# A two-layer trunk of attention and experts: output products gated as a sum, and the mixers' large GpSimd work moved to VectorE

## Chip, cores and metric

The kernel runs on one core of a Trainium2 chip. The metric is the device time of one execution in microseconds (us). A core has five engines that run side by side, each with its own queue in program order: TensorE (PE, matrix products; PEld is its loading of weights), VectorE (DVE), ScalarE (ACT), GpSimd (POOL) and SyncE (SP), which here only issues transfers (DMA). Data lie in SBUF; products come out in PSUM, which has banks of 128 rows by 512 fp32 values. [...]

## Reference

512 positions of width 1024 go through two layers. Each layer is a mixer (layer 0 differential attention, layer 1 banded attention), followed by a mixture of 16 experts, of which each position uses two:

```python
for i in range(DEPTH):
    mod = silu_c @ ada_w[i] + ada_b[i]
    sh1, sc1, g1, sh2, sc2, g2 = [m[:, None, :] for m in jnp.split(mod, 6, axis=-1)]
    h = rms_norm(x, norm_mix_g[i]) * (1.0 + sc1) + sh1
    y = diff_attention(h, ...) if i % 2 == 0 else chunked_attention(h, ...)   # both end in o @ w_o
    x = x + g1 * y
    h = rms_norm(x, norm_ffn_g[i]) * (1.0 + sc2) + sh2
    x = x + g2 * grouped_moe(h, router_w, router_bias, moe_w_gate[i], moe_w_up[i], moe_w_down[i])
```

The products that matter here are `h @ w_qkv` (1024 x 3072), `o @ w_o` (1024 x 1024) with its gate g1, and the adaLN product that gives `mod`. The routing takes sigmoid scores, picks one of four groups of experts and two experts in it.

## The kernel before

All order is written out by hand: the program issues instructions engine by engine in the order of the Python code, and each engine runs its own in that order.

**Weights** arrive as tiles of 128 x 2048 (1 MB) through rings of buffers. `ring.take()` hands out the next tile that has been requested, `ring.done` frees it, and that issues SP's next transfer. To get more than one pass of precision, `split_half` (L330) takes half a tile apart: hi is a copy of reduced precision on ScalarE (L337), lo is the rest, a subtraction (L338) on the engine that `eng` names, VectorE or GpSimd. Three products follow: hi by hi, hi by lo, lo by hi.

**A mixer** walks a list BLOCKS of 12 projection blocks (three for each of four parts q of the heads, L663) and four output blocks ("wo", one for each part, L679). `main_block(n)` runs a block, and at its ticks (every 8 matmuls, or every output group of six) drops in side work: the two splits for the next block, adaLN tiles (`ada_next`), small operations from the lists `bg` and `fin_bg`, and TensorE's transposes of adaLN results from `pe_bg`. Beside it runs `att_stream(q)`, the attention of one part: scores (L747), softmax pieces (VectorE L752, ScalarE L755, VectorE L763 to L775), transposes (L785) and the product with the values (L802, L806). `run_streams` picks which stream goes next by the costs that they yield. Blocks 3 to 11 have the attention of parts 0 to 2 beside them, the output blocks 12 to 14 that of part 3. In layer 0 three output groups are held back to follow it (`held`).

**Engines of the side work.** In the projections one of the two lo parts of a block is GpSimd's, in the output blocks the second one too. The output weights of every part are first multiplied by g1, on GpSimd (L336, two operations of 128 x 1024 per part), so that the products can be added straight to the residual rows `xs` (VectorE, L681): one addition for each part, each of four tiles of rows and each of two column halves, 32 a layer. An adaLN tile is multiplied by the conditioning and accumulated: its first half in one VectorE operation (L431), its second half on ScalarE (L433) and GpSimd (L435). At the layer boundary `first_parts` splits the first weights of layer 1 with both lo parts on GpSimd, while VectorE runs the reciprocal root of the norm (L167 to L173, tiny operations on 128 x 4) and scales the rows (L486); then come the transposes (L538).

**The tail** of a mixer is the output block of part 3 run together with the routing's preparation; then the routing follows, a chain of small VectorE operations with a few small matmuls between (L1082, L1141, L1171), a flag that says whether an expert overflows (a branch, L1389), the gathering of rows and the first expert unit (L1339). The experts' weights come as a stream of 1 MB transfers through three rings.

## Time and profile before

| what | value |
|---|---|
| median of three runs | 1315.2 us (1313.8 to 1316.43) |
| profiled execution | 1313.69 us, span 1311.8 us |
| mean granted clock | 0.947 |
| TensorE busy | 1166.7 us, 89% of the span |
| VectorE, ScalarE, GpSimd busy | 819.5, 617.6, 326.9 us |
| DMA | 327.59 MB, mean 250 GB/s |

The span runs from the first to the last instruction of the profiled execution. Busy times are sums over one engine's instructions; where two engines need each other, the busy shares alone do not tell which sets the time, the idle time before an instruction and its releaser do. The layers lie one after the other: start up to 58 us, layer 0's mixer to 364, routing to 402, experts to 690, layer boundary, layer 1's mixer from 708 to 985, routing, experts to the end.

### The profile page before, as it was taken

What the parts mean: (1) busy time and instruction counts of PE and PEld (TensorE: products, weight loads), DVE (VectorE), ACT (ScalarE), POOL (GpSimd) and SP (SyncE); (2) the same over time, 40 slices, a digit from 0 to 9 for tenths busy, and PEclk for the clock granted to TensorE, in tenths of its full rate; (3) what the DMA queues carried; (4) which work ended last, traced back from release to release, by engine and by line L of the source; (5) the groups of instructions that cost most, each with busy time, mean ns of one, the idle gap of its engine ahead of it and who ended that gap; (6) DMA issues with size and microseconds to landing.
All of it is one profiled execution on the core that took longest, in us unless ns stands there. A gap on an engine that the chain in (4) does not pass through costs nothing. (4 is left out here: it accounts for less than half of the span.)

```text
span 1311.8 us, 19539 instructions
## 1 busy us (share of the span) xinstructions
PE 1166.7 (89%) x7070; PEld 840.4 (64%) x7070; DVE 819.5 (62%) x1800; ACT 617.6 (47%) x1204; POOL 326.9 (25%) x307
## 2 busy tenths in 40 slices
PE   5998899978677999999896999997996899998988
PEld 1677778866565555455576988877775645544565
DVE  3458877779857355254676577856775726544475
ACT  3335556533346254344656455543334634443472
POOL 3114331323242011112103223332525101112211
PEclk7999899989897999999997999998998899999989
DMA  8685565526157699999952343440624879999984
GB/s 291 239 303 215 207 211 192 193 67 230 54 203 298 248 410 404 408 409 410 388 201 77 114 144 112 145 144 33 240 100 179 317 287 402 403 412 403 408 350 138
DMA packets 81937, 327.59 MB, mean 250 GB/s; under 512 B 10663, under 2 KB 35783, under 8 KB 52136
## 3 DMA queue, kind: packets, MB, share of 16 engines
q1 hardware_dynamic: 71176, 302.33, 59.1%
q0 software_dynamic: 10656, 23.93, 7.0%
q8 instruction: 57, 0.93, 0.3%
q14 instruction: 48, 0.39, 0.1%
HBM read 312.53 MB, written 23.15 MB: 256 GB/s over the span
## 5 line engine op out<-in xcount | busy, mean ns | idle before, releaser
L663 PE MATMUL mm<-wlo,hT_hi 128*128 128x256 f32 x704 | 202.9, 288 | 0.8 <-DVE wlo L338 0.8
L663 PE MATMUL mm<-whi,hT_lo 128*128 128x256 f32 x704 | 203.3, 289 | 0.0
L663 PE MATMUL mm<-whi,hT_hi 128*128 128x256 f32 x704 | 202.5, 288 | 0.0
L338 POOL TENSOR_TENSOR wlo<-ring,whi 128x1024 fp32r<-128x1024 f32 x37 | 90.0, 2434 | 375.4 <-ACT whi L337 280.6
L338 DVE TENSOR_TENSOR wlo<-mring,whi 128x1024 fp32r<-128x1024 f32 x116 | 135.6, 1217 | 26.3 <-ACT whi L337 25.6
L755 ACT ACTIVATE p<-p,st 128x128 f32<-128x128 f32 (+3 forms) x128 | 71.0, 555 | 158.4 <-DVE st L752 158.4
L663 PEld LDWEIGHTS mm<-wlo,hT_hi 128*128 128x128 f32 x704 | 135.6, 193 | 12.6 <-issue 9.8
L337 ACT ACTIVATE whi<-mring 128x1024 fp32r<-128x1024 f32 x116 | 119.1, 1056 | 52.2 <-DMA mring<-in_moe_w_gate_dram 20.3
L663 PEld LDWEIGHTS mm<-whi,hT_hi 128*128 128x128 f32 x704 | 135.8, 193 | 5.9 <-issue 2.4
L663 PEld LDWEIGHTS mm<-whi,hT_lo 128*128 128x128 f32 x704 | 135.8, 193 | 5.6 <-issue 4.0
L337 ACT ACTIVATE whi<-ring 128x1024 fp32r<-128x1024 f32 x104 | 107.1, 1049 | 17.7 <-POOLq L1389 6.7
L338 DVE TENSOR_TENSOR wlo<-ring,whi 128x1024 fp32r<-128x1024 f32 x67 | 87.4, 1323 | 44.1 <-ACT whi L337 41.0
L1216 POOL DMA_INDIRECT xb<-y,idx x28 | 56.5, 2016 | 169.0 <-DVE y L1383 94.7
L1210 POOL DMA_INDIRECT hg<-hs,idx x24 | 25.9, 1080 | 283.7 <-DVE wg L1200 129.4
L1301 ACT ACTIVATE hgTf<-tr,mcol 128x128 f32<-128x128 f32 x128 | 48.5, 455 | 88.8 <-PE tr L1296 68.4
L679 PE MATMUL mm<-whi,o 128*128 128x512 f32 x256 | 87.4, 423 | 2.4 <-DVE xs L681 2.1
L1345 PE MATMUL s<-mring,hgTw 128*64 128x512 f32 x224 | 61.2, 614 | 8.2 <-DMA mring<-in_moe_w_up_dram 8.2
L752 DVE CUSTOM_DVE_ANT_0 p<-s,T 128x128 f32<-128x128 f32 (+3 forms) x128 | 57.7, 484 | 13.9 <-PE s L747 12.3
L1339 PE MATMUL mm<-whi,hgTh 128*128 128x512 f32 x128 | 57.6, 450 | 9.6 <-ACT hgTh L1315 9.5
L1376 DVE SCALAR_TENSOR_TENSOR th<-th,s 128x512 f32<-128x512 f32 x24 | 16.4, 684 | 77.4 <-PE s L1345 59.5
L666 ACT ACTIVATE raw<-mm 128x256 f32<-128x256 f32 x88 | 33.0, 376 | 66.8 <-PE mm L663 66.6
L1339 PE MATMUL s<-wlo,hgTh 128*128 128x512 f32 x128 | 52.1, 407 | 8.8 <-DVE wlo L338 8.8
(354 smaller groups left out, 2654.5 us busy)
## 6 DMA issues: line engine op xcount, KB each, us to landing
mring<-in_moe_w_up_dram SPq DMA_DIRECT2D x54, 1024.0 KB, 15.1
mring<-in_moe_w_gate_dram SPq DMA_DIRECT2D x48, 1024.0 KB, 18.4
mring<-in_moe_w_down_dram SPq DMA_DIRECT2D x42, 1024.0 KB, 21.0
ring<-in_ada_w_dram SPq DMA_DIRECT2D x40, 1024.0 KB, 6.6
ring<-in_moe_w_down_dram SPq DMA_DIRECT2D x22, 1024.0 KB, 19.3
ring<-in_moe_w_gate_dram SPq DMA_DIRECT2D x16, 1024.0 KB, 15.5
ring<-in_a_w_qkv_dram SPq DMA_DIRECT2D x24, 512.0 KB, 5.9
ring<-in_b_w_qkv_dram SPq DMA_DIRECT2D x24, 512.0 KB, 5.5
```

Source lines behind the costliest of these rows:

```text
L337: A.activation(hi, raw[:, s], AF.Copy)
L338: eng.tensor_sub(lo, raw[:, s], hi.bitcast(F32))
L663: P.matmul(ps[:, :256], a[:, j, ts_], b[:, w], start=(k == 0), stop=(k == 23))
L666: A.activation(raw[:, t, :], ps[:, :256], AF.Copy)
L679: P.matmul(ps, a[:, j, ts_], b[:, ns], start=(k == 0), stop=(k == 5))
L752: V.tensor_tensor_reduce(out=p[:, :nk], in0=pst[m][:, :nk], in1=T[:, 512 - nk:], scale=-1.0, scalar=3e38, op0=OP.add, op1=OP.min, accum_ou ...
L755: A.activation(p[:, :nk], p[:, :nk], AF.Exp, scale=-1.0, bias=st_[:, m:m + 1], accum_out=st_[:, 2 + m:3 + m])
L1210: G.indirect_dma_start(out=hgs[e % HG], out_offset=None, in_=hs, in_offset=bass.IndirectOffsetOnAxis(ap=idx[:, e:e + 1], axis=0), bounds_c ...
L1216: G.indirect_dma_start(out=xb, out_offset=bass.IndirectOffsetOnAxis(ap=ix[0:n], axis=0), in_=y[0:n], in_offset=None, bounds_check=S - 1, o ...
L1301: A.activation(f, b[:, 128 * (i % 4):128 * (i % 4) + 128], AF.Identity, scale=mcol[:, l, 3, i:i + 1], bias=mcol[:, l, 2, i:i + 1])
L1339: P.matmul(o, a, b, start=(first and i == 0), stop=(last and i == 2))
L1345: P.matmul(b[s, :], lhs[:, s], w[h], start=first, stop=last)
```

## The change

Six things are edited.

1. The output weights' tiles now hold a half of the columns (`wo_item`). A new `wo_block` runs the output products of parts 0 to 2 together: for each column half and each pair of row tiles it opens two banks and adds the 18 matmuls of three parts into each. The sum is multiplied by g1 and added to `xs`, both on VectorE. Splits of the six half tiles are placed at fixed group numbers (`todo`; two of them already in block 11). Only part 3's weights are still multiplied by g1, on VectorE.
2. `split_half` puts lo on VectorE, except where the tail asks for GpSimd. The adaLN tile's second half takes VectorE's one operation too.
3. `first_parts` puts its lo parts off until the rows are scaled.
4. `pe_bg` gets an empty entry, so that adaLN transposes come a tick later; layer 0 does not flush it any more before part 3's attention; seven groups are held back instead of three; tiles of part 3 come from a new pool T["y"].
5. `keep_busy(n)` runs n matmuls 128x512 in fp32 whose result nobody reads, five after the routing's transpose, four after its next-to-last small products.
6. At the routing's end two hi parts come before the overflow flag's branch, and their lo parts after the second gather.

```diff
-            G.tensor_mul(raw[:, s], raw[:, s], scale)
+            r3 = raw[:, s].rearrange("p (j f) -> p j f", j=2)
+            V.tensor_mul(r3, r3, scale[:, None, 512 * k:512 * k + 512].to_broadcast([128, 2, 512]))
         A.activation(hi, raw[:, s], AF.Copy)
-        eng.tensor_sub(lo, raw[:, s], hi.bitcast(F32))
+        if later is None:
+            eng.tensor_sub(lo, raw[:, s], hi.bitcast(F32))
+        else:
+            later.append(lambda: eng.tensor_sub(lo, raw[:, s], hi.bitcast(F32)))
...
-            if k == 0:
-                if j == ej[0]:
-                    V.tensor_scalar(acc[k], w, cj, None, op0=OP.mult)
-                else:
-                    V.scalar_tensor_tensor(acc[k], w, cj, acc[k], op0=OP.mult, op1=OP.add)
+            if j != ej[0]:
+                V.scalar_tensor_tensor(acc[k], w, cj, acc[k], op0=OP.mult, op1=OP.add)
+            elif k:
+                A.activation(acc[k], w, AF.Copy, scale=cj)
             else:
-                A.activation(acc[k] if j == ej[0] else w, w, AF.Copy, scale=cj)
-                if j != ej[0]:
-                    G.tensor_add(acc[k], acc[k], w)
+                V.tensor_scalar(acc[k], w, cj, None, op0=OP.mult)
...
+    def keep_busy(n):
+
+        b = bank("s", 2)
+        for t in range(n):
+            P.matmul(b, ident, xs[:, t % NT, 0:512], start=True, stop=True)
+
+    first_low = []
...
-        parts = [split_half(raw, k, eng=eng) for k in range(2)]
-        ring.done(raw)
+        parts = [split_half(raw, k, later=first_low) for k in range(2)]
+        first_low.append(lambda: ring.done(raw))
...
+        while first_low:
+            first_low.pop(0)()
...
-                if BLOCKS[i][0] == "wo":
-                    parts.append(split_half(raw, k, state["g1"], eng=(G if k else V)))
-                else:
-                    parts.append(split_half(raw, k, eng=(V if k else G)))
+                parts.append(split_half(raw, k, state["g1"] if BLOCKS[i][0] == "wo" else None))
...
+        def wo_block():
+
+            wo_split(2, 0)
+            todo = {3: (0, 1), 8: (1, 1), 10: (2, 1)}
+            nxt = load_split(15)
+            n_y = 0
+            for nb in range(2):
+                ns = slice(512 * nb, 512 * nb + 512)
+                for t2 in range(0, NT, 2):
+                    banks = [bank("mm", 2) for _ in range(2)]
+                    for q in range(3):
+                        hi, lo = wo_parts[q, nb]
+                        ohi, olo = oT[q]
+                        for t, ps in zip((t2, t2 + 1), banks):
+                            ts_ = slice(128 * t, 128 * t + 128)
+                            k = 0
+                            for j in range(2):
+                                w = slice(512 * j, 512 * j + 512)
+                                for a, b in ((ohi, hi), (olo, hi), (ohi, lo)):
+                                    P.matmul(ps, a[:, j, ts_], b[:, w], start=(q == 0 and k == 0), stop=(q == 2 and k == 5))
+                                    k += 1
+                            if q == 2:
+                                V.tensor_mul(ps, ps, state["g1"][:, ns])
+                                V.tensor_add(xs[:, t, ns], xs[:, t, ns], ps)
+                            n_y += 1
+                            bg_step(3)
+                            if pe_bg and n_y % 3 == 0:
+                                pe_bg.pop(0)()
+                            if n_y in todo:
+                                wo_split(*todo[n_y])
+                            if n_y in (14, 22):
+                                nxt[1](n_y // 22)
+                            yield 1300.0
+            state["cur"] = nxt
...
-            held = 3 if l == 0 and n == 4 else 0
+            held = 7 if l == 0 and n == 4 else 0
...
-                while pe_bg:
+                while l and pe_bg:
...
         P.transpose(lgb[:, 0:128], T["lsb"], ident)
+        keep_busy(5)
...
         G.dma_start(g2, bc_row(modd, l * 6 * D + 5 * D, D))
+        keep_busy(4)
         places()
+        low = []
+        split_next(later=low)
+        split_next(later=low)
         overflow()
...
         gather(1)
-        split_next()
-        split_next()
+        for o in low:
+            o()
```

GpSimd's queue at the end of layer 0's mixer, before. `g` is the gate g1, `ring` a weight tile, `T` and `rowsA` the bias rows of the attention; the last rows of lo parts lie in the tail:

```order
L336 TENSOR_TENSOR ring<-ring,g_2455 128x1024 x2
L338 TENSOR_TENSOR wlo<-ring,whi 128x1024
L606 MEMSET T 64x64
L608 DMA T<-rowsA 64x512
L609 DMA T<-rowsA 64x448
L336 TENSOR_TENSOR ring<-ring,g_2455 128x1024 x2
L338 TENSOR_TENSOR wlo<-ring,whi 128x1024
L336 TENSOR_TENSOR ring<-ring,g_2455 128x1024 x2
L338 TENSOR_TENSOR wlo<-ring,whi 128x1024
L336 TENSOR_TENSOR ring<-ring,g_2455 128x1024 x2
L338 TENSOR_TENSOR wlo<-ring,whi 128x1024 x3
```

and at the same place now:

```order
L377 DMA adab<-in_ada_b_dram 4x512
L618 MEMSET T 64x64
L620 DMA T<-rowsA 64x512
L621 DMA T<-rowsA 64x448
L454 DMA modd<-adab 2x512
L618 MEMSET T 64x64
L620 DMA T<-rowsA 64x512
L621 DMA T<-rowsA 64x448
L340 TENSOR_TENSOR wlo<-ring,whi 128x1024 x2
```

The scalings of all parts are gone from GpSimd, and two lo parts, those of the tail, are left; transfers that it issues no longer stand behind large operations.

VectorE's queue in layer 0's output product, before, from one softmax piece of part 3 to the next (L752 reads scores `s`, L763 to L771 mix the two maps):

```order
L681 TENSOR_TENSOR xs<-xs,mm 128x512 x2
L763 RECIPROCAL st<-st 128x2
L767 TENSOR_TENSOR st<-st,nlam 128x1
L769 TENSOR_SCALAR p<-p,st 128x384
L771 SCALAR_TENSOR_TENSOR p<-p,st 128x384
L752 ISA p,st<-s,T 128x512
L752 ISA st 128x1
L752 ISA p,st<-s,T 128x512
L752 ISA st 128x1
```

and now, where a pair of banks closes beside the same kind of pieces:

```order
L669 TENSOR_TENSOR mm<-mm,g_2446 128x512
L670 TENSOR_TENSOR xs<-xs,mm 128x512
L826 RECIPROCAL st<-st 128x2
L830 TENSOR_TENSOR st<-st,nlam 128x1
L832 TENSOR_SCALAR p<-p,st 128x256
L834 SCALAR_TENSOR_TENSOR p<-p,st 128x256
L815 ISA p,st<-s,T 128x384
L815 ISA st 128x1
L815 ISA p,st<-s,T 128x384
L815 ISA st 128x1
L669 TENSOR_TENSOR mm<-mm,g_2446 128x512
L670 TENSOR_TENSOR xs<-xs,mm 128x512
```

The additions, which came in twos between the softmax pieces, have become a multiplication in the bank and an addition for each finished tile, and they come only at the end of every six output groups; a lo part of 128 x 1024 stands between softmax pieces elsewhere in this stretch.

TensorE's queue at the routing, before (`lsb` are the logits, `Mb` the mask of chosen experts):

```order
L1052 MATMUL o<-hTr,rwa 32x128 x8
L1082 MATMUL tr<-ident,lsb 128x128
L1141 LDWEIGHTS before
L1141 MATMUL tr<-Mb,before 128x64
L1143 LDWEIGHTS ones_b
L1143 MATMUL tr<-Mb,ones_b 128x48
```

and now:

```order
L1120 MATMUL o<-hTr,rwa 32x128 x8
L1150 MATMUL tr<-ident,lsb 128x128
L463 MATMUL s<-xs,ident 128x512 x5
L1210 LDWEIGHTS before
L1210 MATMUL tr<-Mb,before 128x64
```

Between the transpose of the logits and the first small product with the mask now stand five matmuls that wait for nothing new.

## Rows read from the trace of the kernel before

**Rows 1.** The page's busy shares: microseconds, share of the span and number of instructions of each engine.

```profile
PE 1166.7 (89%) x7070; PEld 840.4 (64%) x7070; DVE 819.5 (62%) x1800; ACT 617.6 (47%) x1204; POOL 326.9 (25%) x307
```

**Rows 2.** Groups of instructions of the whole run, by line: line, engine, operation, out<-in, shapes, count | busy us, mean ns of one | idle time before them and its releasers. Lo parts, scalings and adaLN additions on GpSimd; then VectorE's own lo parts, its adaLN steps, its additions of output products; then the hi products on TensorE.

```profile
L338 POOL TENSOR_TENSOR wlo<-ring,whi 128x1024 fp32r<-128x1024 f32 x37 | 90.0, 2434 | 375.4 <-ACT whi L337 280.6 <-issue 51.8 <-DVE rq_t L171 30.1
...
L336 POOL TENSOR_TENSOR ring<-ring,g 128x1024 f32<-128x1024 f32 x16 | 39.3, 2478 | 0.2
...
L435 POOL TENSOR_TENSOR o<-o,ring 128x1024 f32<-128x1024 f32 x15 | 38.6, 2572 | 77.1 <-ACT ring L433 65.0 <-issue 6.8 <-PE s L747 5.1
...
L338 DVE TENSOR_TENSOR wlo<-mring,whi 128x1024 fp32r<-128x1024 f32 x116 | 135.6, 1217 | 26.3 <-ACT whi L337 25.6
...
L431 DVE SCALAR_TENSOR_TENSOR o<-ring,csil,o 128x1024 f32<-128x1024 f32 x15 | 22.5, 1498 | 0.0
...
L681 DVE TENSOR_TENSOR xs<-xs,mm 128x512 f32<-128x512 f32 x64 | 43.2, 683 | 23.0 <-PE mm L679 23.0
...
L679 PE MATMUL mm<-whi,o 128*128 128x512 f32 x256 | 87.4, 423 | 2.4 <-DVE xs L681 2.1 <-DVE o L829 0.2
```

**Rows 3.** Timeline of 262 to 284 us (layer 0, last projections beside the third part's attention): start us, duration us, engine, line, operation, out<-in, count, and in brackets the idle time before and its releaser.

```profile
264.68 0.16 DVE L171 TENSOR_TENSOR rq_t<-rq_y,rq_m 128x4 f32<-128x4 f32 x1
...
266.67 4.96 DVE L171 TENSOR_TENSOR rq_t<-rq_y,rq_m 128x4 f32<-128x4 f32 x1
...
266.93 4.68 POOL L336 TENSOR_TENSOR ring<-ring,g 128x1024 f32<-128x1024 f32 x2
...
275.74 1.13 PE L350 MATMUL tr<-ident,adab 128*128 128x128 f32 x4 [7.45 <-DVE qTl L717]
```

**Rows 4.** Busy time of each engine in five stretches: us from the start, length, busy us of PE, PEld, DVE, ACT and POOL with instruction counts, granted clock, DMA share, GB/s. In order: layer 0's projections with attention, its output product with the last attention, the expert stage of layer 0, layer 1's projections, its output product.

```profile
58.00:284.00 226.00, 205.68 (x1596) 171.62 (x1596) 166.57 (x440) 112.19 (x266) 69.68 (x53) 0.95 0.59 208
...
284.00:364.00 80.00, 65.20 (x337) 51.27 (x336) 66.49 (x151) 30.33 (x83) 25.10 (x13) 0.91 0.35 126
...
440.00:640.00 200.00, 185.72 (x904) 100.28 (x903) 94.85 (x178) 84.29 (x139) 30.65 (x20) 0.97 1.00 397
...
708.00:910.00 202.00, 190.57 (x1611) 170.59 (x1611) 138.06 (x334) 103.39 (x224) 63.17 (x64) 0.97 0.37 120
...
910.00:985.00 75.00, 72.29 (x475) 55.90 (x474) 54.83 (x122) 27.94 (x64) 27.16 (x17) 1.00 0.43 155
```

**Rows 5.** Timeline, columns as in rows 3, of 294 to 302, 330 to 346 and 354 to 363 us: layer 0's output product.

```profile
295.24 2.31 DVE L172 SCALAR_TENSOR_TENSOR rq_t<-rq_t,rq_y 128x4 f32<-128x4 f32 x1
...
300.12 0.59 PE L747 MATMUL s<-kTh,qTh 64*128 64x256 f32 x2 [2.18 <-DVE st L752]
...
331.36 2.40 POOL L338 TENSOR_TENSOR wlo<-ring,whi 128x1024 fp32r<-128x1024 f32 x1 [11.70 <-ACT whi L337]
...
336.20 2.29 DVE L171 TENSOR_TENSOR rq_t<-rq_y,rq_m 128x4 f32<-128x4 f32 x1
...
339.08 0.79 PE L785 MATMUL tr<-ident,p 128*128 128x128 f32 x3 [4.32 <-DVE p L771]
...
340.97 1.22 PE L679 MATMUL mm<-whi,o 128*128 128x512 f32 x2 [1.11 <-DVE xs L681]
...
355.12 2.20 DVE L168 TENSOR_SCALAR rq_i<-rq_m 128x4 int32<-128x4 int32 x1
...
360.30 1.17 PE L837 MATMUL tr<-ident,on 128*128 128x128 f32 x4 [4.65 <-DVE on L822]
```

**Rows 6.** Busy time, columns as in rows 4, of four stretches at the lower clock: behind the event of rows 3, in layer 0's output product, and behind the routing of layer 0 and of layer 1.

```profile
271.00:281.00 10.00, 5.26 (x25) 5.27 (x26) 8.32 (x25) 4.76 (x10) 0.60 (x1) 0.50 0.00 0
...
339.00:346.00 7.00, 5.82 (x15) 4.35 (x16) 6.00 (x21) 1.89 (x5) 0.00 (x0) 0.52 0.00 0
...
391.00:407.00 16.00, 9.32 (x45) 7.35 (x46) 10.15 (x38) 8.14 (x16) 3.21 (x4) 0.50 0.58 207
...
1009.00:1021.00 12.00, 5.76 (x37) 4.53 (x38) 8.11 (x30) 4.78 (x10) 3.04 (x3) 0.50 0.60 218
```

**Rows 7.** Timeline, columns as in rows 3, of 688 to 707 us: the boundary from layer 0 to layer 1.

```profile
692.22 4.63 POOL L338 TENSOR_TENSOR wlo<-ring,whi 128x1024 fp32r<-128x1024 f32 x2 [30.06 <-DVE rq_t L171]
...
692.23 2.35 DVE L172 SCALAR_TENSOR_TENSOR rq_t<-rq_t,rq_y 128x4 f32<-128x4 f32 x1
...
694.61 2.27 DVE L173 SCALAR_TENSOR_TENSOR rq_y<-rq_t,rq_y 128x4 f32<-128x4 f32 x1
...
698.94 1.10 PE L538 MATMUL tr<-ident,big 128*128 128x128 f32 x3 [10.38 <-issue]
```

**Rows 8.** Timeline, columns as in rows 3, of 894 to 909 us: the end of layer 1's projections.

```profile
896.36 2.60 DVE L338 TENSOR_TENSOR wlo<-ring,whi 128x1024 fp32r<-128x1024 f32 x1 [3.06 <-ACT whi L337]
...
899.07 2.30 DVE L774 TENSOR_SCALAR p<-p,st 128x384 f32<-128x384 f32 x1
...
901.30 2.49 DVE L775 TENSOR_SCALAR p<-p,st 128x384 f32<-128x384 f32 x1
...
904.17 1.11 PE L713 MATMUL tr<-ident,raw 128*128 128x128 f32 x4 [6.87 <-DVE pT L790]
```

**Rows 9.** First the timeline, columns as in rows 3, of 384 to 408 us (layer 0's routing), then, in the columns of rows 2, the group of fp32 matmuls with 64 rows in the expert stage.

```profile
391.35 0.23 PE L1141 MATMUL tr<-Mb,before 128*128 128x64 f16 x1 [4.95 <-DVE Mb L1138]
...
398.27 0.19 PE L1171 MATMUL tr<-aux,oneh 128*128 128x1 bf16 x1 [5.17 <-DVE oneh L1164]
...
L1345 PE MATMUL s<-mring,hgTw 128*64 128x512 f32 x224 | 61.2, 614 | 8.2 <-DMA mring<-in_moe_w_up_dram 8.2
```

## The prediction

> **What bounds the kernel now.** I read the page first. Its busy shares [rows 1] make TensorE the engine to shorten: busy for 89% of the span, with VectorE at 62% and GpSimd at 25%. The stretches by stage [rows 4] then say where TensorE is not busy. Layer 0's projections (58 to 284 us) leave 226 - 205.7 = 20.3 us, its output product (284 to 364) 14.8, layer 1's projections (708 to 910) 11.4, its output product 2.7. The expert stage from 440 to 640 has its DMA share at 1.00: there the weights' transfers set the pace, and faster arithmetic gives nothing. So what the change can win lies in the mixers, the layer boundary and the routing.

> Next I looked at what TensorE waits for in those gaps, in the timeline. The longest one [rows 3] shows the pattern. A tiny VectorE operation on a 128x4 tile, which takes 0.16 us a little earlier, takes 4.96 us at 266.67, exactly while GpSimd runs two large multiplies (266.93, 4.68 us). Behind it stand softmax pieces, and TensorE stands idle 7.45 us until 275.74. The same happens at 295, 331 to 340 and 355 [rows 5], at the layer boundary [rows 7] and in layer 1 at 899 [rows 8]. VectorE is not short of time; it is held while a large GpSimd operation with operands in SBUF runs. The additions that read PSUM do not show it: 64 of them have a mean of 683 ns [rows 2]. After such a gap the granted clock is at its lower level for some microseconds [rows 6], so that a gap costs more than its length.

> **GpSimd's large work goes.** GpSimd runs 37 lo parts of 2.43 us, 16 scalings of 2.48 and 15 adaLN additions of 2.57: 90.0 + 39.3 + 38.6 = 168 us [rows 2]. By the order of the changed kernel 5 of the 37 remain, 2 in each tail and one at the start. VectorE takes over 32 lo parts, the nearest row being its own lo parts of 1.22 us, and 15 adaLN steps, of which its own like step takes 1.50 with the blocking in it: 32 x 1.22 + 15 x 1.22 to 1.50 = 57 to 62 us. It also takes 4 scalings of the last part's weights (4 x 1.2 to 1.5, about 5). The output products of three parts, 48 additions, become 16 multiplies and 16 additions, 16 operations of 0.683 fewer: -11. Net about +54 us on VectorE. In the four mixer stretches it is busy 166.6 + 66.5 + 138.1 + 54.8 = 426 of 583 us [rows 4]; with 54 more it is at 82%, even if no blocked microsecond came back. So the added work has room on average; what it costs where it stands in front of a softmax piece is bounded by one lo part, 1.2 us, against the 2.3 to 5 us that stand there now.

> Place by place:
> - Event at 268 [rows 3]: the held operation ends 4.96 - 0.16 = 4.8 us earlier, and TensorE's gap falls from 7.45 to about 2.6. The 10 us behind it ran at clock 0.50 with 5.26 us busy, worth 2.6 at full clock [rows 6]; I take 1.2 of it, since a gap stays. Gain 6 (bounds 3 to 10).
> - Layer 0's output product [rows 5]: gaps of 2.2 us at 300, 4.3 + 1.1 at 339 and 341 with 2.9 us of low clock behind (half of 5.82 busy at 0.52, [rows 6]), and 4.65 at 360: 15.2 in all. The last one is the end of the attention: VectorE's chain there is held 2.2 us of it, and seven groups instead of three are now kept back for that place. What remains late is the reciprocal root chain itself and the two operations per finished tile (below); I leave 3.2. Gain 12 (bounds 0 to 16).
> - Other gaps of layer 0's projections: 20.3 - 7.5 = 12.8 us left. They are short waits for softmax pieces, with the same cause in those I opened, but VectorE gets about 20 of the new operations there. I take half, 6 (bounds -3 to 13; the lower end is twenty operations of 1.2 us of which one in eight hits).
> - Layer boundary [rows 7]: two operations of the root chain take 2.35 and 2.27 us beside GpSimd's 4.63; unheld they take 0.16 each, so 4.3 come off a chain with nothing beside it: TensorE waits 10.38 us for its end. The lo parts come after the scaling of the rows, before the weights are wanted. Gain 4 (3 to 5).
> - Layer 1 at 899 [rows 8]: two operations of 2.30 and 2.49 would take some 0.5 each, a lo part of 2.60 would take 1.22, one more lo part comes: 3.8 + 1.4 - 1.2 = 4. With one of clock, 5 (2 to 8) of a gap of 6.87. The other gaps there are 11.4 - 6.9 = 4.5; a third, 1.5 (-2 to 4). Layer 1's output product has 2.7 us of gaps at full clock; 0.5 (-4 to 2).
> - Start, the one early lo part aside: 0.5.

> **The tails.** The lo parts left on GpSimd hold VectorE again, as the one before 355.12 did for 2.20 us [rows 5]. [...] The sum has nothing for the tails.

> **Output products in one bank.** The matmuls are the same in number and shape. New is that two tiles' banks stay open over six groups of six matmuls, and that each is free only after a multiply and an addition, 2 x 0.683 us, at 4 places per layer. While the second bank's last group of six runs, VectorE can finish the first, so on time the wait is near nothing; behind one lo part it is 1.2 us. 8 places x 0 to 2.5 us: I put 2 us of it into the 3.2 above, the rest into the half microsecond of layer 1. In the kernel before, TensorE waited only 2.1 us in 256 matmuls on these additions [rows 2].

> **Kept busy at routing.** Two gaps stand in the routing chain, 4.95 us before L1141 and 5.17 before L1171 [rows 9]; behind them 16 us have clock 0.50 in layer 0 with 9.32 busy, and 12 us in layer 1 with 5.76 [rows 6]. If the clock stayed up, up to 4.7 + 2.9 = 7.5 us would come back. The trace has no full fp32 matmul of 128 rows; the nearest is a 64-row one of 614 ns [rows 9]. Five are then 3.1 us and four 2.5: inside the gaps, but 1.9 and 2.7 us stay empty, and at half clock the five take 6.1 and push L1141 back by 1.2. Bounds -2.4 to 7.5; I take 3, nearer the middle, because an idle time remains in each gap. The hi parts that now come ahead of the overflow branch are ScalarE work beside this and change the end by nothing that I can see.

> **Sum.** 6 + 12 + 6 + 4 + 5 + 1.5 + 0.5 + 0.5 + 3 = 38.5 us. The expert stages shift with the routing, since their stream starts from buffers that free up there. The profiled execution took 1313.7 us (span 1311.8 and 1.9 around it): 1275.2. The median of the three runs is 1.5 higher, so 1276.

> **Rivals.**
> Half only: the gaps pass to the next releaser. For it: in each event a softmax piece, a transpose and a copy stand behind the held operation, and VectorE at 82% will at times have a lo part or a 1.5 us adaLN step in front. Against: the gaps named by row sum to 31 us, and in each the held time is read off directly. 19 us, 1295.
> All of it: the gaps of the four stretches (49) and the boundary (10), with half of the low-clock busy time (2.6 + 2.9 + 4.7 + 2.9 = 13), are 72 us. If only what hangs on true dependences stays, some 12, the gain is 60: 1254. For it: one cause stands behind all the gaps I opened. Against: the boundary's chain and the routing's remain.
> Slower: the bank pairs. If VectorE comes late to the multiply at each of the 8 places by what one lo part and a softmax pair take (2.3 us), and each gap is followed by low clock as at 339 (2.9), they cost 8 x 5.2 = 42; by the whole gap of that place, 4.3, it is 8 x 7.2 = 58. Against 38.5 + 2 that ends at 1315 to 1333, in the middle 1323. It decides from about 5 us a place. For it: VectorE is busy 66.5 of 80 us in this stretch already. Against: TensorE's 2.1 us named above, and the blocks that made VectorE late are gone. [...]
> Nothing: the removed work was covered after all, and the time stays within 0.2%, 2.6 us, which is what a measurement here can tell from no change. Against it stand all the rows on held operations.

> **Chances.** Forecast 0.52, with its own range 1264 to 1288; half 0.22; all 0.16; slower 0.07; nothing 0.03. The range runs from 1252 (all) to 1301 (half with the lower bounds of the unknown costs). Faster 0.90, same 0.03, slower 0.07.

> **What would show it.** In the profile after: no VectorE operation on a 128x4 tile above 0.3 us outside the tails; GpSimd's busy time down by about 150 us; TensorE idle in the first projections below 12 us; its first transpose at the boundary about 6 us after its last matmul there instead of 10.4; clock above 0.8 in the 16 us behind the routing. I am wrong if the waits in the output product are now for the multiply by the gate, if VectorE's lo parts head the list of releasers in the projections, or if the clock behind the routing is still 0.50.

## The result and the profile after

The changed kernel takes 1278.74 us (median of four runs, 1276.95 to 1280.16) against 1315.82 us (four runs, 1313.8 to 1316.77): a ratio of 0.972, 95% interval 0.9702 to 0.9737, so 37 us less. The forecast was 1276 us. The profiled execution has a span of 1275.2 us and a mean granted clock of 0.965 instead of 0.947, as shares of full speed. One of the four runs of the kernel of experiment 4 took 1631.33 us at a mean granted clock of 0.648 and is left out of its median.

The page's busy shares after, which answer to [rows 1]:

```profile
span 1275.2 us, 19476 instructions
PE 1171.8 (92%) x7106; PEld 835.2 (65%) x7106; DVE 788.4 (62%) x1835; ACT 601.1 (47%) x1189; POOL 171.4 (13%) x244
```

TensorE's busy time is 5 us longer, 18.0 us of fillers included, in a span that is 36.6 us shorter. GpSimd's busy time fell by 155 us, VectorE's by 31 in spite of the operations that it took over.

The groups of instructions after, columns as in [rows 2], which they answer to: the lo parts that GpSimd kept, VectorE's lo parts from the ring, its adaLN steps, the multiplication by the gate and the addition, the hi products on TensorE, and the fillers:

```profile
L340 POOL TENSOR_TENSOR wlo<-ring,whi 128x1024 fp32r<-128x1024 f32 x5 | 12.3, 2453 | 171.9 <-ACT whi L338 171.9
...
L340 DVE TENSOR_TENSOR wlo<-ring,whi 128x1024 fp32r<-128x1024 f32 x93 | 112.7, 1225 | 74.0 <-ACT whi L338 73.5
...
L433 DVE SCALAR_TENSOR_TENSOR o<-ring,csil,o 128x1024 f32<-128x1024 f32 x30 | 37.0, 1279 | 0.0
...
L669 DVE TENSOR_TENSOR mm<-mm,g 128x512 f32<-128x512 f32 x16 | 11.1, 696 | 5.8 <-PE mm L666 5.8
...
L670 DVE TENSOR_TENSOR xs<-xs,mm 128x512 f32<-128x512 f32 x16 | 11.0, 687 | 0.5
...
L666 PE MATMUL mm<-whi,o 128*128 128x512 f32 x192 | 61.9, 404 | 1.6 <-DVE xs L670 1.5
...
L463 PE MATMUL s<-xs,ident 128*128 128x512 f32 x36 | 18.0, 649 | 0.0
```

VectorE's lo parts from the ring are 93 instead of 67, but their mean went from the 1323 ns of the kernel before to 1225; its adaLN steps doubled in number and went from 1498 ns to 1279. Counting every VectorE instruction that took at least 0.4 us more than the quickest quarter of the same operation and shape, the excess was 80.7 us in 43 instructions before, and is 1.3 in one, which stands at the start beside the early lo part. So VectorE lost 79 us of being held and took over some 48 us of work, for which the prediction's sum has 54.

**Where the time came from.** Below are stage lengths, from the first matmul of a stage to the first of the next, read off both traces. The way from the boundary's first transpose to layer 1's first projection product, 3.3 us in both, is not in the table, nor is the end behind the experts of layer 1.

| stage | before | changed | gain | forecast |
|---|---|---|---|---|
| layer 0 projections | 258.6 | 247.9 | 10.7 | 12 |
| layer 0 output product and tail | 94.8 | 84.8 | 10.0 | 12 |
| layer 0 routing, to the first expert product | 15.3 | 14.7 | 0.6 | 3 for both routings |
| layer 0 experts and boundary | 297.6 | 294.4 | 3.2 | 4 |
| layer 1 projections | 222.3 | 213.6 | 8.7 | 6.5 |
| layer 1 output product and tail | 79.4 | 76.0 | 3.4 | 0.5 |
| layer 1 routing | 15.0 | 14.8 | 0.2 | with layer 0 |
| layer 1 experts | 286.5 | 286.4 | 0.1 | 0 |

The start, for which 0.5 us was forecast, gave nothing: the first projection product stands at 32.7 us instead of 32.6.

The same stretches by busy time after, columns as in [rows 4]: projections, output product, experts of layer 0, then of layer 1:

```profile
32.70:280.70 248.00, 233.73 (x1815) 191.68 (x1814) 175.01 (x490) 116.59 (x285) 15.74 (x35) 0.98 0.62 216
280.70:365.50 84.80, 75.99 (x413) 59.34 (x412) 60.29 (x167) 35.73 (x94) 15.56 (x35) 0.98 0.42 161
380.20:674.60 294.40, 266.48 (x1244) 160.23 (x1244) 161.30 (x285) 145.97 (x241) 45.22 (x38) 0.96 0.90 352
677.90:891.40 213.50, 208.87 (x1770) 187.52 (x1769) 147.21 (x375) 105.97 (x233) 15.90 (x40) 0.98 0.35 116
891.40:967.40 76.00, 75.25 (x460) 57.88 (x458) 50.78 (x120) 30.36 (x72) 15.55 (x35) 1.00 0.48 180
982.20:1268.60 286.40, 265.50 (x1243) 160.18 (x1244) 156.05 (x267) 138.07 (x222) 43.96 (x30) 0.97 0.89 350
```

TensorE now lacks 14.3, 8.8, 27.9, 4.6, 0.8 and 20.9 us of being busy. Outside the experts 28.5 us of gaps are left; the two expert stretches, at a DMA share of 0.90 and 0.89, are as long as before but for the boundary.

The event of [rows 3], at its new place in the timeline of 258 to 270 us:

```profile
260.63 0.16 DVE L171 TENSOR_TENSOR rq_t<-rq_y,rq_m 128x4 f32<-128x4 f32 x1
...
266.36 0.55 PE L848 MATMUL tr<-ident,p 128*128 128x128 f32 x3 [2.73 <-DVE qTl L780]
```

The 128x4 operations take 0.16 us, and TensorE's gap is 2.73 us where it was 7.45. What is late now is the chain of copies itself (ScalarE's qTh, then VectorE's qTl). The boundary of [rows 7], timeline of 667 to 684 us:

```profile
672.17 0.17 DVE L172 SCALAR_TENSOR_TENSOR rq_t<-rq_t,rq_y 128x4 f32<-128x4 f32 x1
672.37 0.16 DVE L173 SCALAR_TENSOR_TENSOR rq_y<-rq_t,rq_y 128x4 f32<-128x4 f32 x1
...
674.61 1.15 PE L548 MATMUL tr<-ident,big 128*128 128x128 f32 x3 [6.10 <-DVE big L497]
...
675.13 2.35 DVE L342 TENSOR_TENSOR wlo<-ring,whi 128x1024 fp32r<-128x1024 f32 x2
```

10.38 us became 6.10. The two lo parts stand behind the scaling of the rows, and delay nothing: from the first transpose to the first projection product it takes 3.28 us, and took 3.29 before.

### The profile page after: what moved, and what is told of

Same layout as the page of the kernel before. It is cut to its first block, busy times and chain, and to the rows that moved or that the text cites. A ratio compares the mean times of both kernels' runs of the same rounds, so it can differ in the third digit from the quotient of the medians.

```text
span 1275.2 us, 19476 instructions
## 1 busy us (share of the span) xinstructions
PE 1171.8 (92%) x7106; PEld 835.2 (65%) x7106; DVE 788.4 (62%) x1835; ACT 601.1 (47%) x1189; POOL 171.4 (13%) x244
## 5 line engine op out<-in xcount | busy, mean ns | idle before, releaser
L340 DVE TENSOR_TENSOR wlo<-ring,whi 128x1024 fp32r<-128x1024 f32 x93 | 112.7, 1225 | 74.0 <-ACT whi L338 73.5
L725 PEld LDWEIGHTS mm<-wlo,hT_hi 128*128 128x128 f32 x704 | 134.2, 191 | 12.9 <-issue 10.4
L1408 PE MATMUL mm<-whi,hgTh 128*128 128x512 f32 x128 | 56.1, 439 | 11.4 <-ACT hgTh L1384 11.2
L666 PE MATMUL mm<-whi,o 128*128 128x512 f32 x192 | 61.9, 404 | 1.6 <-DVE xs L670 1.5
L1408 PE MATMUL mm<-whi,hgTl 128*128 128x512 f32 x128 | 54.6, 426 | 5.2 <-DVE hgTl L1385 5.2
```

What stands on the lines that cost most here:

```text
L340: eng.tensor_sub(lo, raw[:, s], hi.bitcast(F32))
L666: P.matmul(ps, a[:, j, ts_], b[:, w], start=(q == 0 and k == 0), stop=(q == 2 and k == 5))
L725: P.matmul(ps[:, :256], a[:, j, ts_], b[:, w], start=(k == 0), stop=(k == 23))
L1408: P.matmul(o, a, b, start=(first and i == 0), stop=(last and i == 2))
```

## Experiments

Medians are compared with the changed kernel's 1278.74 us; where stages are named, with the table above. The stage of layer 0's output product was 84.8 us in the changed kernel's profile and 86.7 to 86.9 in seven other profiles of kernels that do not touch it, so 2 us there are scatter of one execution: the granted clock of the stage was 0.98 in the changed kernel's profile, and 0.96 in those of `dummy_pool_adds` and `no_keep_busy`. By the usual 86.8 the stage's gain is 8.0 us and not 10.0.

**1. A GpSimd operation that nobody needs.** Behind the first lo part of every projection block:

```diff
+                if k == 0 and BLOCKS[i][0] == "qkv":
+                    G.tensor_add(raw[:, 0:1024], raw[:, 0:1024], raw[:, 0:1024])
```

> The changed kernel with one large GpSimd addition (128x1024, two SBUF inputs) put behind the lo part of each first half tile of the projections, into a weight half that nobody reads any more; only the ring's next transfer waits for it. VectorE's own work stays as it is. Theory A: a large GpSimd operation holds VectorE's operations on SBUF while it runs, whoever needs its result; 22 of them cost 6 to 15 us, and VectorE operations on 128x4 or 128x16 tiles of 2 us and more appear beside them. Theory B: what cost time before was waiting for GpSimd's results or their place in the order; as nobody waits for these, the time changes by less than 1.5 us and no VectorE operation is longer.

1311.05 us, 32.3 more: layer 0's projections 261.5 us (+13.6), layer 1's 233.4 (+19.8), all else unchanged. Theory A holds, and at 6 to 15 us its price was put too low by more than half. Expectations below call the hold of VectorE beside a large GpSimd operation, which this run shows, the lock. In the timeline of 872 to 878 us:

```profile
873.53 2.13 DVE L839 TENSOR_SCALAR p<-p,st 128x384 f32<-128x384 f32 x1
873.56 1.89 POOL L526 TENSOR_TENSOR ring<-ring 128x1024 f32<-128x1024 f32 x1 [7.09 <-issue]
...
876.25 0.68 DVE L817 CUSTOM_DVE_ANT_0 p<-s,T 128x512 f32<-128x512 f32 x1
```

An operation that usually takes 0.42 us took 2.13, until GpSimd was done. 21 such are held by 30.0 us in all. TensorE's idle time grows by 7.6 and 11.0 us in the two stages, its time at the lower clock by 10 and 18 us. With half of that time taken as lost, the two together are 33 us; the half is an estimate from the kernel before, where projection products of 128x256 followed each other every 0.21 us at a granted clock of 0.50 (278 to 281 us) and every 0.12 us at 1.00 (850 to 856 us). TensorE's waits in both stages end on VectorE for the most part (2.5 us in layer 1 on a ScalarE hi part); on a DMA it waits 0.4 us, so the later release of the weight buffer plays no part that shows.

**2. The same places with fills.**

```diff
+                    for _ in range(2):
+                        G.memset(raw[:, 0:1024], 0.0)
```

> As the dummy additions (which took 1311.05 us), but each of the 22 is replaced by two GpSimd fills of 128x1024 into the same dead half, about 0.95 us each: GpSimd is busy as long at the same places, and the ring's transfer waits as long, but nothing is read from SBUF. Theory A (VectorE is held by GpSimd operations that read SBUF): the time stays within 2 us of the changed kernel's 1278.7, no VectorE operation is stretched. Theory B (the cost of the dummy additions came from the later release of the ring's buffer, or from GpSimd's queue being late): the time is as with the additions, 1300 or more.

1289.56 us, 10.8 more (layer 0's projections +4.7, layer 1's +11.1 in the profiled execution, which at 1293.66 us was the slowest of four). Neither theory: a third of the additions' cost remains, and VectorE is held by 15.2 us in 21 instructions (1.3 of it in the one of the changed kernel). The weight buffers are released as late as with the additions (the two fills below take 1.98 and 2.00 us, the addition above 1.89), so that is not the cause. Which ones is what tells. In the timelines of 219 to 222 and 755 to 760 us:

```profile
218.72 1.98 POOL L527 MEMSET ring<- 128x1024 f32 x2 [22.92 <-DVE wlo L340]
220.04 1.23 DVE L340 TENSOR_TENSOR wlo<-ring,whi 128x1024 fp32r<-128x1024 f32 x1 [0.24 <-ACT whi L338]
...
756.77 1.10 DVE L840 TENSOR_SCALAR p<-p,st 128x256 f32<-128x256 f32 x1
756.77 2.00 POOL L527 MEMSET ring<- 128x1024 f32 x2 [10.06 <-issue]
757.79 1.12 DVE L841 TENSOR_SCALAR p<-p,st 128x256 f32<-128x256 f32 x1
```

The subtraction, with two inputs in SBUF, went through beside the fills in its usual 1.23 us; L840 and L841, with a single tensor input, from SBUF to SBUF, took 1.10 and 1.12 instead of 0.35, each to about the end of a fill. So A's condition, that GpSimd must read SBUF, was too narrow: which instruction was held depended on both operations (last section).

**3. Part of GpSimd's work put back.** First the lo parts of the projections:

```diff
-                parts.append(split_half(raw, k, state["g1"] if BLOCKS[i][0] == "wo" else None))
+                parts.append(split_half(raw, k, state["g1"] if BLOCKS[i][0] == "wo" else None, eng=(V if k or BLOCKS[i][0] == "wo" else G)))
```

> The changed kernel with the lo part of each first half tile of the projections on GpSimd again, 22 operations; adaLN, output products and all else as changed. Theory A (the lock): VectorE has 27 us less to do but is held for up to 53 us, and the time rises by 5 to 12 us, most of it in the two projection stretches. Theory B (VectorE's load sets the pace now): it falls by 1 to 4 us.

1281.19 us, 2.5 more; the projections are 251.5 and 214.4 us (+3.6, +0.8). The sign is A's, the size below it: VectorE is held 24.5 us, but is rid of 27 us of its own. Then the second halves of the adaLN tiles:

```diff
+            if j != ej[0] and not k:
...
+            elif k:
+                A.activation(acc[k] if j == ej[0] else w, w, AF.Copy, scale=cj)
+                if j != ej[0]:
+                    G.tensor_add(acc[k], acc[k], w)
```

> The changed kernel with the second halves of the adaLN tiles as before: ScalarE multiplies, GpSimd adds (15 operations of 128x1024). Theory A: these, not the lo parts (which cost only 2.5 us when put back), made most of the projections' gaps, because VectorE works on the same tile's first half and on softmax pieces at that time: plus 5 to 10 us, in layer 0 above all, where 10 of the 15 are. Theory B: as with the lo parts, VectorE gives away as much work as it is held, and the time changes by less than 3 us; then only both together make the gaps of before.

1289.32 us, 10.6 more; the projections are 255.7 and 216.7 us (+7.8, +3.1). Theory A. 15 operations cost four times what 22 lo parts do, with less held time (21.5 us). VectorE is rid of work here too, 15 steps of 1.28 us, so the microseconds held and given away do not explain the difference. An adaLN addition comes beside VectorE's step on the same tile, and ScalarE gets 15 multiplications more; which of the two counts, no run shows. Then both, and the early lo parts of layer 1, and one of two lo parts in the output products:

```diff
-            wo_parts[q, nb] = split_half(wo_raw[q], nb)
+            wo_parts[q, nb] = split_half(wo_raw[q], nb, eng=(G if nb else V))
...
-        parts = [split_half(raw, k, later=first_low) for k in range(2)]
-        first_low.append(lambda: ring.done(raw))
+        parts = [split_half(raw, k, eng=G) for k in range(2)]
+        ring.done(raw)
```

> The changed kernel with GpSimd's lo parts (one of two in projections and output products), adaLN additions and the first lo parts of layer 1 as before; only the weight scalings stay off it, and the output products are still added up in one bank. Theory A (the costs add, stage by stage): the two projection stretches are longer by 3.6 + 7.8 and 0.8 + 3.1 us as in the two runs apart, the boundary by 4, the output products by 2 to 6: 1298 to 1304, so that the sum in one bank keeps some 12 us against before without the lock being gone. Theory B (only all held operations together made the gaps of before): 1308 or more.

1293.32 us, 14.6 more. Stage by stage:

| stage | changed | lo parts | adaLN | all three |
|---|---|---|---|---|
| layer 0 projections | 247.9 | 251.5 | 255.7 | 257.4 |
| layer 0 output product | 84.8 | 86.9 | 86.7 | 86.8 |
| layer 1 projections | 213.6 | 214.4 | 216.7 | 216.4 |
| layer 1 output product | 76.0 | 76.0 | 76.0 | 75.8 |

The projections' costs add up to four fifths of the two apart in layer 0 (9.5 of 11.4) and 2.8 of 3.9 in layer 1; the boundary's stage is longer by 2.3. Theory A's sum, 1298 to 1304, was too high above all by the output products, where the lo parts on GpSimd cost nothing. In layer 1's projections 2.8 us come back of the 8.7 gained. What is not put back are the scalings of the weights: in the kernel before, two of them (L336, 897.84 to 903.57 us) ran beside two of the held operations of [rows 8], as L336 did in the event of [rows 3].

**4. The hold gone, the sum in one bank not made.** The kernel before with

```diff
-            G.tensor_mul(raw[:, s], raw[:, s], scale)
+            V.tensor_mul(raw[:, s], raw[:, s], scale)
...
-                    parts.append(split_half(raw, k, state["g1"], eng=(G if k else V)))
+                    parts.append(split_half(raw, k, state["g1"]))
...
-                    parts.append(split_half(raw, k, eng=(V if k else G)))
+                    parts.append(split_half(raw, k))
...
-    def first_parts(eng=G):
+    def first_parts(eng=V):
```

and the adaLN tiles as in the change.

> The kernel before with the mixers' large GpSimd work (lo parts, weight scalings, second halves of the adaLN tiles, the first lo parts of layer 1, not put off) on VectorE and nothing else changed: output products still added part by part. Theory A: the lock alone explains the gain, so this gets at least 25 of the 37 us, 1284 to 1291. Theory B: without the sum in one bank VectorE has 20 us more work in the output products (16 scalings of 1.2 us, and 16 additions more than the changed kernel), which shows there, and at most 15 us come, 1300 or more.

1302.44 us (three runs, 1302.19 to 1305.6), ratio 0.9909 (0.989 to 0.9928): 12 to 13 of the 37 us, theory B. The stretches of this kernel in the order of the changed kernel's above, of which the second and the fifth are the output products:

```profile
33.50:280.00 246.50, 234.06 (x1814) 192.69 (x1813) 176.42 (x492) 116.16 (x284) 15.82 (x35) 0.97 0.62 217
280.00:375.60 95.60, 80.26 (x412) 61.41 (x410) 69.94 (x180) 37.08 (x94) 15.57 (x35) 0.93 0.38 143
...
692.40:905.90 213.50, 208.87 (x1770) 187.50 (x1769) 147.95 (x375) 104.05 (x230) 15.92 (x40) 0.98 0.34 112
905.90:993.60 87.70, 77.88 (x461) 58.09 (x459) 61.31 (x134) 32.34 (x75) 15.57 (x35) 1.00 0.40 156
```

The projections are 246.6 and 213.5 us, as short as in the changed kernel: there the move off GpSimd explains the whole gain. The boundary's stage is 298.2 us against 297.6 before: on VectorE, but not put off, the first lo parts cost what the hold had cost. The output products are 95.6 and 87.7, no shorter than before in layer 0 and 8.3 longer in layer 1. VectorE is busy there 69.9 and 61.3 us against 60.3 and 50.8 in the changed kernel: it has all 16 scalings, of which the changed kernel keeps four (so 12 more, not the 16 of the expectation), and 64 additions, where the changed kernel has 32 additions and 16 multiplications. TensorE's waits in layer 1's output product (905.9 to 993.6 us), of which the changed kernel has neither:

```profile
PE o L803 <- DVE pT L787: 4.3, 3, 1.6
PE mm L676 <- DVE xs L678: 3.0, 4, 1.4
```

This kernel lacks more than the sum in one bank: the attention of part 2 is finished a step later beside that of part 3 (`wait` is 3 where the changed kernel has 2, an edit that the list of the change does not name), the output weights are split by rows and not by columns, and in layer 0 three groups are held back and the adaLN transposes are flushed. Of these only the held groups were tested alone (experiment 6).

**5. Banks one after the other.**

```diff
-                for t2 in range(0, NT, 2):
-                    banks = [bank("mm", 2) for _ in range(2)]
+                todo_ts = [(0, 1), (2,), (3,)] if nb == 0 else [(t,) for t in range(NT)]
+                for grp in todo_ts:
+                    banks = [bank("mm", 2) for _ in grp]
```

> The changed kernel with the output products one bank after the other (18 matmuls into each) from the second pair of row tiles on, instead of two banks side by side; the same matmuls and VectorE operations. Theory A (banks in pairs cost little, as VectorE can finish the first while the second gets its last six): within 1.5 us. Theory B (the pairs make TensorE wait for both banks): 2 to 5 us faster, and the waits of L666 for L670, 1.5 us in all now, go to nothing.

1289.17 us, 10.4 more: the output products are 93.1 and 78.9 us. Neither theory had this sign. VectorE's waits in layer 0's output product, 280 to 362 us, first after the change, then here (who waited for whom: us in total, times, longest):

```profile
DVE wlo L340 <- ACT whi L338: 6.4, 5, 2.0
...
DVE mm L669 <- PE mm L666: 4.4, 2, 4.0
```

```profile
DVE wlo L340 <- ACT whi L338: 8.8, 5, 4.3
DVE mm L670 <- PE mm L667: 8.3, 3, 5.9
```

and in the timeline of 300 to 309 us of this kernel

```profile
303.96 1.23 DVE L340 TENSOR_TENSOR wlo<-ring,whi 128x1024 fp32r<-128x1024 f32 x1 [4.34 <-ACT whi L338]
...
305.10 0.69 DVE L670 TENSOR_TENSOR mm<-mm,g 128x512 f32<-128x512 f32 x1
...
308.24 0.90 PE L849 MATMUL tr<-ident,p 128*128 128x128 f32 x4 [2.95 <-DVE p L835]
```

VectorE stands 4.34 us in front of a lo part whose hi part waited for a buffer that the running group of 18 matmuls still reads, then does the multiplication and the addition; the softmax piece behind them comes late, and TensorE waits 2.95 us for it. With pairs, TensorE waits 1.5 us for L670 in this stage, and no more than that shows there. The other order moves VectorE's waits to worse places; as the lo parts are placed by group number, they stand elsewhere among the groups, and the run does not tell the two apart.

**6. Groups held back.**

```diff
-            held = 7 if l == 0 and n == 4 else 0
+            held = 3 if l == 0 and n == 4 else 0
```

> The changed kernel with three instead of seven output groups held back behind the attention of layer 0. Theory A, the prediction's: TensorE waits for the end of the attention by some 3 us more at the last transposes (L900) and the clock falls there, plus 3 to 5 us in layer 0's output product. Theory B: without GpSimd's large operations the chain is so much shorter that four groups more or less do not show: under 1 us.

1277.94 us, no difference, theory B. TensorE's longest wait for the last transposes is 5.8 us here and 3.0 in the changed kernel, but their sum is 6.7 against 5.5, and the stage has 85.2 us against 84.8.

**7. No fillers at the routing.**

```diff
-        keep_busy(5)
...
-        keep_busy(4)
```

> The changed kernel without the nine filler matmuls at each of the two routings. Theory A, the prediction's term: the clock behind the routing falls to 0.50 again for some 16 and 12 us, and the time rises by about 3 us (up to 7.5), to 1281.7 from 1278.7. Theory B: the first expert unit is paced by VectorE's lo parts and by the weights, not by TensorE, so that the lower clock comes back but the time rises by no more than 1 us. In both the granted clock behind L1150 falls; the stretch from the routing's first transpose to the layer boundary tells them apart: longer by 1.5 us or more per layer under A, under 0.5 under B.

1280.01 us, 1.3 more, which the spread of the runs does not tell from nothing; theory B. The clock does what A says. Busy time and granted clock of the 16 us from 10.2 us before the first expert product of layer 0, of the next 16, and of the 12 us from some 11 us before that of layer 1, first with fillers, then without:

```profile
370.00:386.00 16.00, 11.99 (x58) 7.70 (x58) 10.67 (x40) 7.05 (x15) 3.37 (x4) 0.89 0.57 195
386.00:402.00 16.00, 11.99 (x63) 9.26 (x62) 13.68 (x22) 11.24 (x19) 3.79 (x5) 0.86 0.99 410
971.00:983.00 12.00, 9.27 (x44) 4.31 (x42) 9.08 (x36) 3.61 (x8) 3.05 (x3) 0.86 0.67 239
```

```profile
373.00:389.00 16.00, 9.47 (x50) 7.42 (x51) 10.26 (x37) 6.59 (x15) 3.36 (x4) 0.57 0.54 188
389.00:405.00 16.00, 11.75 (x62) 9.10 (x61) 13.67 (x22) 11.23 (x19) 3.81 (x5) 0.86 1.01 419
974.00:986.00 12.00, 4.24 (x33) 3.25 (x33) 9.42 (x37) 3.49 (x7) 2.94 (x3) 0.50 0.68 233
```

0.89 and 0.86 became 0.57 and 0.50. But the stage from the first expert product to the boundary takes 294.6 us without and 294.4 with them, in layer 1 286.3 and 286.4. The clock is given back and buys nothing that shows. That fits a stage which goes by its transfers: in the second 16 us the DMA share is 0.99 and 1.01.

**8. The boundary.** The lo parts not put off:

```diff
-        parts = [split_half(raw, k, later=first_low) for k in range(2)]
-        first_low.append(lambda: ring.done(raw))
+        parts = [split_half(raw, k) for k in range(2)]
+        ring.done(raw)
```

> The changed kernel with the first lo parts of layer 1 not put off, on VectorE ahead of the scaling of the rows. Theory A: they stand in the boundary's chain, 2 x 1.22 us and the wait for ScalarE's hi parts, plus 2.5 to 4.5 us between the last expert product and the first transpose. Theory B: they fit beside ScalarE's squares, under 1 us.

1282.78 us, 4.0 more; in the profiled execution the stage with the boundary is 3.6 us longer (298.0 against 294.4): theory A.

**9. The tail's lo parts on VectorE.**

```diff
-        ast, tail = mixer(l, on_half, on_x, before_tail, 2 * [lambda: split_next(G)], first)
+        ast, tail = mixer(l, on_half, on_x, before_tail, 2 * [lambda: split_next(V)], first)
```

> The changed kernel with the two lo parts of each tail on VectorE as well, so that GpSimd has one large operation left in the whole run. Theory A (the lock): VectorE is held 2 x 2.3 us a tail less and has 2 x 1.22 more to do; the output stretches get up to 2 us shorter each, 1275 to 1278. Theory B: TensorE runs the tail at 96% and more already, so it hides this: within 1 us of 1278.7.

1286.08 us, 7.3 more: both theories miss the sign. The output stages are 90.8 and 80.0 us (+4 over the usual 86.8, and +4.0), and the experts of layer 1 take 288.7 (+2.3). TensorE's waits in the tail of layer 0 begin with two that the changed kernel does not have:

```profile
PE tr L1092 <- DVE xs L744: 2.0, 1, 2.0
PE o L1120 <- DVE hTr L1096: 1.3, 1, 1.3
```

A lo part that VectorE must wait for (1.80 us for its hi part) stands ahead of the additions and copies that the routing's products need. And theory A had nothing to win: in the changed kernel GpSimd's lo parts of the tails hold no VectorE instruction. In its timeline of 345 to 354 us, layer 0's tail, the additions (from the bank `mm`) and the copies (from the bank `tr`) take their usual 0.69 and 0.68 us beside them:

```profile
345.61 2.39 POOL L340 TENSOR_TENSOR wlo<-ring,whi 128x1024 fp32r<-128x1024 f32 x1 [80.01 <-ACT whi L338]
346.35 0.69 DVE L744 TENSOR_TENSOR xs<-xs,mm 128x512 f32<-128x512 f32 x1 [0.42 <-PE mm L742]
346.95 0.68 DVE L1096 COPY hTr<-tr 128x512 f32<-128x512 f32 x1
```

Here GpSimd is the better place.

**10. A better version.** The longest gap left in layer 0's projections, in the changed kernel's timeline of 143 to 151 us:

```profile
149.35 0.22 DVE L358 SCALAR_TENSOR_TENSOR mcol<-tr,gffn 128x4 f32<-128x4 f32 x2
...
149.72 1.09 PE L848 MATMUL tr<-ident,p 128*128 128x128 f32 x4 [5.14 <-DVE mcol L358]
```

The transposes of an adaLN result hold one of two banks until VectorE copies them out. The adaLN sums' own bank is free by then:

```diff
+        cb = bank("ada", 1)
         pe_bg.append(lambda: None)
-        pe_bg.append(lambda: cols(l, mr, [(i, h, q + h) for i, q in at for h in range(2)]))
+        pe_bg.append(lambda: cols(l, mr, [(i, h, q + h) for i, q in at for h in range(2)], cb))
```

(`cols` uses that bank for its transposes.)

> The changed kernel with the transposes of the adaLN results in the bank that the adaLN sums just left, instead of one of the two banks of the softmax transposes. In the changed kernel the longest gap left in layer 0's projections, 5.1 us at 144, is a softmax transpose (L848) that waits for VectorE's copies out of the adaLN transposes (L358), which stand behind VectorE's other work. Theory A: the gap is the bank's alone; it shrinks to 2 us or less and the time falls by 2 to 5 us, 1274 to 1277. Theory B: VectorE is late by that much for every consumer, so the wait passes to the softmax piece behind it or to the next adaLN sums (L413), and the time stays within 1.5 us.

1276.33 us, 2.4 less than the changed kernel; ratio to before 0.9695 (0.968 to 0.971), an interval that overlaps the changed kernel's, so the gain is not clear of the spread. Layer 0's projections take 245.4 us (-2.5). Of the 5.1 us, 2.4 are left as a wait for a 128x16 operation and 1.3 at the next adaLN sums:

```profile
PE tr L849 <- DVE rq_m L167: 2.4, 1, 2.4
...
PE ada L413 <- issue: 1.3, 1, 1.3
```

So 1.4 us of the gap are gone with the bank, and 2.4 have passed to a wait for late work of VectorE; what the 1.3 us wait for, the profile does not show.

## Why the prediction was right, and where not

The bound was read rightly: TensorE's gaps in the mixers and the boundary, made by VectorE instructions that a large GpSimd operation held (80.7 us of excess before, 1.3 after), and nothing in the experts. The first experiment shows the hold (30.0 us in 21 instructions) with an operation that has no consumer, and the fourth shows that the move off GpSimd gives the whole gain in the projections.

By its steps:

- Event at 268: gap forecast at 2.6, measured 2.73 (before another transpose, with the same releaser). Layer 0's projections 10.7 against 12, layer 1's 8.7 against 6.5: right within the bounds of each.
- Layer boundary: forecast 4, 10.38 became 6.10, and experiment 8 takes 4.0 back. Right; it needs both edits, off GpSimd and put off, as experiment 4 shows.
- Layer 0's output product: 10.0 in the profile, 8.0 by the usual 86.8, against 12: within the bounds, but wrong in cause. The step said that the gaps of 15.2 us go because the hold goes. Experiment 4 has none of the scalings and lo parts on GpSimd there, but for the tail's, and gains nothing; the last kernel of experiment 3 has four lo parts of each layer's output products on GpSimd, which hold VectorE by 2.8 us in layer 0 (17.4 before), and loses nothing. What the runs showed in its place: without the hold the stretch gets no shorter while VectorE has the scalings and the additions part by part to do. The changed kernel takes 32 of the 48 additions and 12 of the 16 scalings away for 16 multiplications, and VectorE is busy about 10 us less in each layer than in experiment 4. That the rest comes from this and not from the other edits named there is argued from these busy times and waits and not shown by a run. The text counted the additions as "-11" in VectorE's sum and put the effect on the time at a loss of 2.
- Layer 1's output product: forecast 0.5 (-4 to 2), measured 3.4, outside these bounds, and probably for the same reason. TensorE's 3.3 us of gaps there are now 0.8.
- Seven groups held back: named as part of the gain of 12; experiment 6 shows no effect.
- Routing: forecast 3, measured 1.3 at most, from experiment 7, and the stages say 0.8 for both together. The failed step is "If the clock stayed up, up to 4.7 + 2.9 = 7.5 us would come back". The clock did come back; that the stage behind it belongs to the transfers, which the first paragraph of the prediction says of 440 to 640 us, fits from the first expert product on (294.6 us without fillers, 294.4 with them). The filler's price was low too: five took 4.46 us, not 3.1, and still fitted. The 614 ns that it was read from are one record, and a filler shows as two (36 records for 18 fillers). And the trace of before does have fp32 matmuls of 128 rows: L1546, 128x512, 56 records in 26.1 us.
- Tails: nothing was put into the sum, and the profile shows none, but not for the reason given. "The lo parts left on GpSimd hold VectorE again" is the step that failed: they hold no instruction, and the additions and copies of 128x512 that run beside them, which read PSUM, take their usual 0.68 to 0.69 us in both tails (experiment 9).
- Of the rivals, half and all of it did not come. The slower one, bank pairs, did not either: TensorE waits 1.5 us for L670. Layer 1's output product, with banks in pairs too, ran at a granted clock of 1.00, with 0.8 us of idle time. The rivals' 31 us of gaps named by row count the boundary at 4.3 us; at its whole 10.38 they are 37.
- Signs: those on 128x4 operations, on GpSimd, on the boundary and on the clock came true. TensorE idles 12.7 us from 58 us to the end of the first projections, where below 12 was asked; it was 20.3. None of the three signs of being wrong came.

That the sum came out within 3 us owes something to luck: the routing's 2 us too many and layer 0's mixer 3 too many (5 by the usual output stage) stand against 5 too few in layer 1's.

## What to carry to other kernels

Read an instruction's duration against its own kind: the 128x4 operations of 2 to 5 us on VectorE were not slow but held (0.16 us elsewhere, 4.96 at the longest, [rows 3]), and the line beside them on GpSimd told by what. Before moving such work to the held engine, look at what it would stand in front of: the same lo parts were worth 2.5 us moved out of the softmax's way in the projections, and 7.3 us left on GpSimd in the tail; and best is to do without the operation, as the gate on the sum does. A clock that is kept up need not be worth time: behind layer 0's routing 0.89 instead of 0.57 left the expert stage at 294.4 us against 294.6, with a DMA share of 0.99 in the 16 us from 386 us on.

## What the runs showed of the hardware

Second, the price of a hold was not its length. 30.0 us of held VectorE time cost 32.3 us behind VectorE's own lo parts, 15.2 us beside the fills cost 10.8, and 24.5 us only 2.5 where the hold replaced work of VectorE. What the time was made of is TensorE's gaps and the lower clock behind them: beside the additions, in layer 1's projections, 11.0 us more of idle time brought 17.5 us more at the lower clock.
